# One head layout for the operands of the RWKV chunk products, halves exchanged by the stores, and a wider search for the issue order

## Chip, cores and metric

The kernel runs on one core of a Trainium2 chip. The time is the device time of one execution in microseconds. A core has five engines that run side by side, each through its own instructions in order: PE (TensorE, matmuls), DVE (VectorE), ACT (ScalarE), POOL (GpSimd) and SP (SyncE, which here only issues DMAs; ACT issues some too).

## The reference, cut to what matters

One decoder layer over T = 1024 tokens of width 1024, all in float32: a normalised input goes through one projection; its columns feed three head groups (8 RWKV-7 heads, 4 heads of sparse attention, 4 heads of attention over 256 memory tokens); their outputs go through one output projection.

```python
h = rms_norm(x, norm_in_g[l]); p = h @ w_in[l]
p_rwkv, p_nsa, p_mem = jnp.split(p, [...], axis=-1)
# RWKV-7, per head, token by token, S is a 64x64 state:
sa = jnp.einsum('bhvk,bhk->bhv', S, -kk_t)
S = (S * w_t[:, :, None, :] + sa[..., None] * (kk_t * a_t)[:, :, None, :]
     + v_t[..., None] * k_t[:, :, None, :])
y = jnp.einsum('bhvk,bhk->bhv', S, r_t)
# sparse attention and memory attention on their columns, then
x = x + jnp.concatenate([y_rwkv, y_nsa, y_mem], axis=-1) @ w_out[l]
return rms_norm(x, norm_final_g)
```

## The kernel before, in words

**Recording and ordering.** The program is written as generators. They don't issue instructions: `nc.vector`, `nc.tensor` and so on only record them. `ordered` then takes the whole list and chooses one order for all engines and queues, and issues it; every recorded instruction thus has the line of the call in `ordered` (L574). It goes through 30 turns. Each turn gives buffers to tiles in the order of the last turn (`_slots`), builds the dependences (`_edges`), ranks every instruction by the modelled time from it to the end (`_backward`), and lays the list out anew on modelled engines, highest rank first (`_forward`). The order whose modelled end is earliest is issued. At run time each engine follows its list strictly.

**Stages.** (1) x comes in as 8 tiles of 128 tokens (tiles `A_84` to `A_89`), is normalised and transposed into two halves `H`; a projection tile is `pa<-H,wh` and `pa<-H,wl`: 24 matmuls on a weight tile that was loaded raw (`wr`, one buffer), rounded by ACT (`wh`) and its rest taken by POOL or DVE (`wl`). (2) RWKV: `decay` and `elementwise` run for 8 units, head pair hp = 0 to 3 times half h of the tokens. Partitions 0 to 63 hold the even head of a pair, 64 to 127 the odd one. A unit makes xr (scaled kk and r, 128 columns for each of 8 chunks of 64 tokens) and bk (scaled b and k), multiplies them on PE head by head (64x128 tiles), masks the products into W and transposes bk into bt. All goes by DMA to `st_d` in DRAM, per chunk in four slots of 128 columns: 0 and 1 the operands for the state, 2 the chunk's own products, 3 bt. (3) `inverse(pr)` for head pairs 0, 1 (pr = 0, tile `A_336`) and 2, 3 (pr = 1, tile `A_480`): slot 2 is loaded as 128 small triangles, a substitution of 31 steps runs on DVE (a product `P4<-A` and a sum `A<-A,P4` each), ACT turns the result round, it goes through `md` and `nd` in DRAM, four passes of 32x32 matmuls join the triangles (pr = 1: `pa_539`, `pa_537`), and the result is stored to slot 2. (4) `chunks`: 16 chunks in sequence, each loading a 1 MB tile `C<-st_d`; per chunk PE makes px (`ch<-T,C`), ACT copies it (`xe`), PE makes pq (`ch<-xe,C`), DVE and ACT copy it, PE makes pn and DVE forms the next state. The first chunk is `ch_555<-T2_550,C_549`. Other work (memory attention, projections, sparse attention) is laid between these by the order. (5) The rest of the sparse attention and the output projection.

In the unit, the operands of the odd head have their two halves of 64 columns swapped (`halves`), so that each head's result lies on the partitions where the state needs it; all elementwise instructions there work on 64 partitions, and there are two masks, `MK[0]` and `MK[1]`.

Of the kernel before, what the change touches and what calls it, by code (L numbers as in the profile page):

```python
# [14 lines left out]
OP = mybir.AluOpType  # L15
# [382 lines left out]
def _backward(ops, preds, first):  # L398
# [15 lines left out]
    while done < n:  # L414
        best = None
        for e in engines:
            w, a = wait[e], able[e]
            while w and w[0][0] <= free[e]:
                k = heapq.heappop(w)[1]
                heapq.heappush(a, (-first[k], k))  # L420
            at = free[e] if a else w[0][0] if w else None
            if at is not None and (best is None or at < best[0]):
                best = at, e
        at, e = best
        if not able[e]:
            free[e] = at
            continue
        k = heapq.heappop(able[e])[1]
        o = ops[k]
        R[k] = max(floor[k], at + o.occ)  # L430
        free[e] = at + o.occ
        done += 1
        for p, same in preds[k].items():
            q = ops[p]
            d = 0.0 if same == 2 else q.occ if same else q.took + LAG[o.e] + MARGIN
# [8 lines left out]
def _forward(ops, preds, after, rank, phase):  # L444
# [20 lines left out]
    while done < n:  # L465
        if forced is not None:
            k, e, at = forced, "PE", free["PE"]
        else:
# [13 lines left out]
            if e == "PE" and prev is not None and len(able[e]) > 1:  # L482
                a = able[e]
                m = _mode(prev)
                k = min(a, key=lambda x: (x[0] + SWITCH * (_mode(ops[x[1]].shape) != m), x[1]))
# [55 lines left out]

MARGIN = 150.0
# [6 lines left out]
ROUNDS = 30  # L549


def ordered(tc, ops, log=None):
# [3 lines left out]
    seq = list(range(len(ops)))  # L556
    best, start = None, seq
    for n in range(ROUNDS):
        at = {k: n for n, k in enumerate(seq)}
# [3 lines left out]
        rank = _backward(ops, preds, start)  # L563
        rank = [r + max(0.0, FIRST - k) * 1e3 for k, r in enumerate(rank)]
        order, start, end = _forward(ops, preds, after, rank, 1100.0)
        if log is not None:
            log(n, late, end)
        seq = sorted(range(len(ops)), key=lambda k: (start[k], k))
        if best is None or end < best[0]:
            best = end, seq  # L570
# [9 lines left out]
def build(tc, x, mem, w_in, w_gl, w_kv, w_out, lora, pv_d, rows_d, cst_d, rope_d, w1_d, pos_d, w2_d, out):  # L580
# [3 lines left out]
    with ctx:  # L584
# [178 lines left out]
        MK = [maskb[:, K_MK + 128 * q:K_MK + 128 * q + 128] for q in range(2)]  # L763
# [180 lines left out]
        def elementwise(hp, h):  # L944
# [28 lines left out]
            halves = [(slice(64 * q, 64 * q + 64), 64 * q, 64 - 64 * q) for q in range(2)]  # L973
            for q, (r, ac, rc) in enumerate(halves):
                (V, G)[q].tensor_mul(xr[r, :, rc:rc + 64], r4[r], gg[r, :, 1:65])
                G.tensor_mul(bk[r, :, rc:rc + 64], p4_[r], gi4[r])
# [16 lines left out]
            for r, ac, rc in halves:  # L993
                V.scalar_tensor_tensor(xr[r, :, ac:ac + 64], k4[r], -1.0, gg[r, :, 0:64], op0=OP.mult, op1=OP.mult)
                V.scalar_tensor_tensor(bk[r, :, ac:ac + 64], b4[r], 0.5, gi4[r], op0=OP.mult, op1=OP.mult)
# [10 lines left out]
            for d in range(2):  # L1006
# [908 lines left out]
```

## Time and profile before

| | |
|---|---|
| time, median of 3 runs | 779.72 us (778.71 to 779.91) |
| profiled execution, its own time | 783.57 us |
| its span | 781.8 us |
| PE busy | 728.4 us, 93% |
| DVE, ACT, POOL busy | 540.4, 389.5, 342.6 us |
| DMA packets | 124744, of which 50816 under 512 B |

The profile is of one execution, 3.85 us longer than the median. An engine's busy share is over all stages; which wait counts in a stage is read from the idle time of PE there and what ended it. PEclk is the clock granted to PE, as a share of the full one.

### The profile page before, as it was taken

The numbers are of one execution on the slowest core, as the hardware profiler recorded it, in microseconds if no ns is written. First come the engines' busy times: TensorE is split into PE (matmuls) and PEld (weight loads), VectorE is DVE, ScalarE is ACT, GpSimd is POOL, SyncE is SP. The second block draws the span as 40 slices with busy tenths as digits, with TensorE's granted clock in tenths as the row PEclk, the third lists the DMA queues.
The fourth block names the chain that finished last, engine by engine and source line by source line (L and its number), as shares of the span: only waits on it lengthen the run. The fifth ranks groups of instructions, "written<-read, shape, count | busy, mean of one in ns | idle before, by whom it ended". The sixth has DMA issues, their size and how long they took to land.

```text
span 781.8 us, 15135 instructions
## 1 busy us (share of the span) xinstructions
PE 728.4 (93%) x5736; PEld 596.8 (76%) x5738; DVE 540.4 (69%) x1044; ACT 389.5 (50%) x854; POOL 342.6 (44%) x370
## 2 busy tenths in 40 slices
PE   2899999999999999779988999999998999999996
PEld 2888887888888878667766776777776888888885
DVE  4963658578888787744579868668898777666532
ACT  4653345263553222543567555453686675765541
POOL 3644416454273013120365656555243145255664
PEclk9999999999999998979999999999999999999998
DMA  8212574756757777598466675533251021121112
GB/s 338 77 32 62 124 191 105 179 133 176 190 128 192 207 160 123 164 163 281 150 203 203 195 243 178 176 109 106 91 162 61 8 75 36 54 81 62 55 55 80
DMA packets 124744, 105.67 MB, mean 135 GB/s; under 512 B 50816, under 2 KB 108544, under 8 KB 122496
## 3 DMA queue, kind: packets, MB, share of 16 engines
q1 hardware_dynamic: 108096, 95.57, 43.6%
q10 hardware_dynamic: 16576, 9.14, 4.3%
q8 instruction: 45, 0.74, 0.4%
q14 instruction: 27, 0.22, 0.1%
HBM read 68.52 MB, written 36.18 MB: 134 GB/s over the span
## 4 chain that ended last, share of the span: by engine, by line
PE 67%; DVE 12%; DMA 11%; ACT 3%; POOL 3%; issue 2%; SPq 0%; ACTq 0%; DVEq 0%; POOLq 0%
PE pa L574 47%; PE ch L574 20%; DVE A L574 4%; DVE T L574 2%; DMA A<-in_x_dram 2%; DMA yd<-S 2%; DVE S L574 1%; DVE P L574 1%; DVE wst L574 1%; DMA st_d<-A 1%; DMA S<-nd 1%; DMA C<-st_d 1%; DVE N L574 1%; DMA S<-g_d 1%; DMA wr<-in_w_out_dram 1%
## 5 line engine op out<-in xcount | busy, mean ns | idle before, releaser
L574 PE MATMUL pa<-H,wh 128*128 128x512 f32 (+1 forms) x928 | 292.5, 394 | 4.4 <-DVE H L574 1.7
L574 PEld LDWEIGHTS pa<-H,wh 128*128 128x128 f32 x928 | 170.7, 190 | 39.1 <-DVE H L574 2.1
L574 PE MATMUL pa<-H,wl 128*128 128x512 f32 (+1 forms) x464 | 180.6, 392 | 1.3 <-POOL wl L574 1.3
L574 POOL TENSOR_TENSOR wl<-wr,wh 128x1024 fp32r<-128x1024 f32 x27 | 66.1, 2447 | 104.6 <-ACT wh L574 96.2
L574 PE MATMUL ch<-H,C 128*128 128x512 f32 x360 | 104.4, 408 | 0.6 <-POOL H L574 0.4
L574 PEld LDWEIGHTS pa<-H,wl 128*128 128x128 f32 x464 | 88.1, 190 | 19.4 <-POOL wl L574 1.6
L574 ACT ACTIVATE S<-pa 128x512 fp32r<-128x512 f32 (+4 forms) x112 | 58.5, 544 | 44.6 <-PE pa L574 32.6
L574 PE MATMUL pa<-A 64*64 64x64 f32 (+4 forms) x416 | 74.6, 307 | 2.5 <-DVE A L574 1.7
L574 PEld LDWEIGHTS ch<-H,C 128*128 128x128 f32 x360 | 63.2, 189 | 9.7 <-POOL H L574 0.8
L574 ACT ACTIVATE wh<-wr 128x1024 fp32r<-128x1024 f32 x32 | 33.9, 1059 | 65.0 <-PE pa L574 43.1
L574 DVE TENSOR_REDUCE wst<-pa 128x1 f32<-128x384 f32 (+3 forms) x96 | 47.6, 516 | 16.4 <-PE pa L574 15.9
L574 PEld LDWEIGHTS pa<-A 128*128 128x128 f32 (+1 forms) x416 | 51.5, 175 | 9.2 <-issue 2.8
L574 DVE TENSOR_TENSOR N<-pa,S 128x512 fp32r<-128x512 f32 (+1 forms) x76 | 45.4, 615 | 13.0 <-ACT S L574 11.3
L574 PEld LDWEIGHTS ch<-T,C 128*64 128x64 f32 (+1 forms) x1008 | 33.6, 136 | 15.8 <-issue 6.2
L574 POOL TENSOR_TENSOR sgc<-T,gc 64x256 f32<-64x256 f32 x30 | 20.5, 683 | 56.3 <-DVE T L574 55.0
L574 PE MATMUL ch<-T,C 128*64 128x64 f32 (+1 forms) x1008 | 39.4, 226 | 5.0 <-ACT T L574 1.5
L574 DVE SCALAR_TENSOR_TENSOR T<-ch,gc,sgc 64x64 f32<-64x64 f32 x120 | 33.9, 283 | 13.1 <-PE ch L574 6.1
L574 ACT ACTIVATE T<-pa,pv 128x512 f32<-128x512 f32 x34 | 23.1, 681 | 34.3 <-PE pa L574 23.7
L574 ACT ACTIVATE NP<-pa,wst 128x384 f32<-128x384 f32 (+3 forms) x52 | 29.0, 564 | 19.2 <-DVE wst L574 10.9
L574 PE MATMUL pa<-cst,NP 128*128 128x128 f32 x212 | 33.6, 278 | 3.2 <-ACT NP L574 1.5
L574 POOL TENSOR_TENSOR S<-S,N 128x512 f32<-128x512 f32 x8 | 10.3, 1290 | 57.5 <-DVE N L574 39.1
L574 PEld LDWEIGHTS pa<-cst,NP 128*128 128x128 f32 x212 | 25.7, 142 | 9.6 <-ACT NP L574 2.8
(207 smaller groups left out, 1483.0 us busy)
## 6 DMA issues: line engine op xcount, KB each, us to landing
C<-st_d SPq DMA_DIRECT2D x16, 1024.0 KB, 5.6
wr<-in_w_in_dram SPq DMA_DIRECT2D x28, 512.0 KB, 3.9
st_d<-C SPq DMA_DIRECT2D x32, 256.0 KB, 4.7
st_d<-A SPq DMA_DIRECT2D x24, 256.0 KB, 3.6
A<-in_x_dram SPq DMA_DIRECT2D x8, 512.0 KB, 7.5
st_d<-NP SPq DMA_DIRECT2D x8, 512.0 KB, 5.5
P<-in_x_dram SPq DMA_DIRECT2D x8, 512.0 KB, 3.4
out_dram<-P SPq DMA_DIRECT2D x7, 512.0 KB, 2.6
```

The source lines that it names most:

```text
L574: i = o.call(*o.args, **o.kw).ins
```

## The change

In `elementwise`, xr and bk keep the same order of columns for both heads. Every 64-partition pair of instructions becomes one of 128 partitions: per unit, four multiplications (one on DVE, three on POOL) become two on POOL, and four scalar_tensor_tensor on DVE become two. One mask serves both heads. Since the products of the odd head then lie with halves swapped, the stores put them right: seven stores per unit become twelve, most of them of 64 columns (256 bytes in a row) where they were of 128 (512 bytes). The matmuls are the same in number and form.

In `ordered`, 150 turns replace 30. From turn 12 on, the ranks get random noise, the margin and the price of changing PE's tile size are drawn at random, and every second turn starts from the best order so far. What is best is judged no more by the modelled end of the layout but by `_replay`: the fixed order is played through the model three times with random slack on every duration, and the mean end counts.

```diff
@@ -546,28 +609,43 @@
-ROUNDS = 30
+ROUNDS = 150
+CHAIN = 12
+SEED = 0
+SPREAD = 0.06
+NOISE = 50.0
+AGAIN = 2
 
...
     users, tags = _tiles(ops)
-    seq = list(range(len(ops)))
-    best, start = None, seq
-    for n in range(ROUNDS):
-        at = {k: n for n, k in enumerate(seq)}
+    n, rng = len(ops), np.random.RandomState(SEED)
+    slacks = [(1 + SPREAD * np.abs(rng.randn(n)) * np.array([1 + 2 * (o.dma is not None) for o in ops])).tolist() for _ in range(3)]
+    seq = first = list(range(n))
+    best = None
+    for turn in range(ROUNDS):
+        if turn >= CHAIN and turn % AGAIN == 0:
+            seq, first = best[1], best[2]
+        at = [0] * n
+        for m, k in enumerate(seq):
+            at[k] = m
         taken = {t: sorted(names, key=lambda x: min(at[k] for k in users[x])) for t, names in tags.items()}
         took, late = _slots(users, taken, seq)
         preds, after = _edges(ops, users, took)
-        rank = _backward(ops, preds, start)
-        rank = [r + max(0.0, FIRST - k) * 1e3 for k, r in enumerate(rank)]
-        order, start, end = _forward(ops, preds, after, rank, 1100.0)
+        loose = turn >= CHAIN
+        add = NOISE * rng.randn(n) * loose
+        rank = _backward(ops, preds, first, MARGIN * (2 * rng.rand() if loose else 1.0))
+        rank = [r + max(0.0, FIRST - k) * 1e3 + a for (k, r), a in zip(enumerate(rank), add.tolist())]
+        order, start, end = _forward(ops, preds, after, rank, 1100.0, SWITCH * (2 * rng.rand() if loose else 1.0))
+        first, seq = start, sorted(range(n), key=lambda k: (start[k], k))
+        tries = [_replay(ops, preds, after, seq, 1100.0 * (m + 1), x) for m, x in enumerate(slacks)]
+        score = sum(x[0] for x in tries) / len(tries)
         if log is not None:
-            log(n, late, end)
-        seq = sorted(range(len(ops)), key=lambda k: (start[k], k))
-        if best is None or end < best[0]:
-            best = end, seq
+            log(turn, late, end, score)
+        if best is None or score < best[0]:
+            best = score, seq, first
     last = {}
     for k in best[1]:
         o = ops[k]
-        MK = [maskb[:, K_MK + 128 * q:K_MK + 128 * q + 128] for q in range(2)]
+        MK = maskb[:, K_MK:K_MK + 128]
         gc = const.tile([128, 4, 16], F32, name="gc")
...
             bk = NP((128, 8, 128))
-            halves = [(slice(64 * q, 64 * q + 64), 64 * q, 64 - 64 * q) for q in range(2)]
-            for q, (r, ac, rc) in enumerate(halves):
-                (V, G)[q].tensor_mul(xr[r, :, rc:rc + 64], r4[r], gg[r, :, 1:65])
-                G.tensor_mul(bk[r, :, rc:rc + 64], p4_[r], gi4[r])
+            G.tensor_mul(xr[:, :, 64:128], r4, gg[:, :, 1:65])
+            G.tensor_mul(bk[:, :, 64:128], p4_, gi4)
             yield 0.86, 0.0
 
             pvv = bank("ch")
...
             k4, b4 = ch(kn), ch(ba)
-            for r, ac, rc in halves:
-                V.scalar_tensor_tensor(xr[r, :, ac:ac + 64], k4[r], -1.0, gg[r, :, 0:64], op0=OP.mult, op1=OP.mult)
-                V.scalar_tensor_tensor(bk[r, :, ac:ac + 64], b4[r], 0.5, gi4[r], op0=OP.mult, op1=OP.mult)
+            V.scalar_tensor_tensor(xr[:, :, 0:64], k4, -1.0, gg[:, :, 0:64], op0=OP.mult, op1=OP.mult)
+            V.scalar_tensor_tensor(bk[:, :, 0:64], b4, 0.5, gi4, op0=OP.mult, op1=OP.mult)
             yield 0.43, L_BONUS
             pbn = bank("pa")
...
-                    V.tensor_mul(W[:, q, c4], pe[q], MK[q].unsqueeze(1).to_broadcast([128, 4, 128]))
+                    V.tensor_mul(W[:, q, c4], pe[q], MK.unsqueeze(1).to_broadcast([128, 4, 128]))
                 yield 1.1, L_MASK
-            for q in range(2):
-                r, o = slice(64 * q, 64 * q + 64), slice(64 - 64 * q, 128 - 64 * q)
-                nc.sync.dma_start(st_d[r, cl, 2, hp, :], W[r, q])
-                nc.sync.dma_start(st_d[o, cl, q, hp, :], W[o, q])
-                nc.sync.dma_start(st_d[r, cl, q, hp, :], xr[r])
-            nc.sync.dma_start(st_d[:, cl, 3, hp, :], bt)
+
+            u, d, both = slice(0, 64), slice(64, 128), (slice(0, 64), slice(64, 128))
+            nc.sync.dma_start(st_d[u, cl, 2, hp, :], W[u, 0])
+            nc.sync.dma_start(st_d[d, cl, 0, hp, :], W[d, 0])
+            nc.sync.dma_start(st_d[u, cl, 0, hp, :], xr[u])
+            for a, b in (both, both[::-1]):
+                nc.sync.dma_start(st_d[d, cl, 2, hp, b], W[u, 1, :, a])
+                nc.sync.dma_start(st_d[u, cl, 1, hp, b], W[d, 1, :, a])
+                nc.sync.dma_start(st_d[d, cl, 1, hp, b], xr[d, :, a])
+                nc.sync.dma_start(st_d[a, cl, 3, hp, d], bt[b, :, d])
+            nc.sync.dma_start(st_d[:, cl, 3, hp, u], bt[:, :, u])
 
         def rwkv():
             yield ("lora",)

```

The new `_replay` in its core:

```python
def _replay(ops, preds, after, seq, phase, slack):
    ...
    for k in seq:
        ...
        s = max(r, free[e])
        gap[k], why[k] = s - free[e], w if r >= free[e] else before[e]
        ...
        free[e], before[e] = c, k
        start[k], fin[k] = s, (s, f, c)
        if f > end:
            end, tail = f, k
    return end, gap, why
```

What the change does to the order is shown at three places. A name such as pa_562 is a PSUM tile; the number is the same in both kernels.

The first place is SP's queue at the start of the program, before:

```order
L574 DMA A_84<-in_x_dram 128x1024 x2
L574 DMA A_87<-in_x_dram 128x1024
L574 DMA wr_86<-in_w_in_dram 128x1024
L574 DMA A_87<-in_x_dram 128x1024
L574 DMA A_88<-in_x_dram 128x1024 x2
L574 DMA A_89<-in_x_dram 128x1024 x2
L574 DMA P4_152<-in_lora_dram 128x1024
L574 DMA wr_156<-in_w_in_dram 128x1024
```

and after:

```order
L652 DMA A_84<-in_x_dram 128x1024 x2
L652 DMA wr_86<-in_w_in_dram 128x1024
L652 DMA A_87<-in_x_dram 128x1024 x2
L652 DMA A_88<-in_x_dram 128x1024 x2
L652 DMA A_89<-in_x_dram 128x1024 x2
L652 DMA P4_152<-in_lora_dram 128x1024
L652 DMA wr_156<-in_w_in_dram 128x1024
```

The raw weight tile `wr_86` of the first projection now stands ahead of the third tile of x, not behind it. (A_87, A_88 and A_89 are the later pairs of tiles of x.)

The second place is PE at the four passes of 32x32 matmuls of the second inverse (`pa_539`, `pa_537`; `A_480` is its tile). Here is a piece of before, around the third and fourth pass (the first two stand further ahead in it, one in the midst of pa_562 and one in the midst of pa_548):

```order
L574 MATMUL pa_548<-H_104,wl_546 128x512
L574 MATMUL pa_548<-H_104,wh_547 128x512
L574 MATMUL pa_539<-A_480,S2_531 32x32 x32
L574 MATMUL pa_548<-H_105,wh_547 128x512
L574 MATMUL pa_548<-H_104,wl_546 128x512
L574 MATMUL pa_548<-H_104,wh_547 128x512
L574 MATMUL pa_537<-A_480,S2_530 32x32 x32
L574 MATMUL pa_548<-H_105,wh_547 128x512
L574 MATMUL pa_548<-H_104,wl_546 128x512
```

and of after:

```order
L652 MATMUL pa_603<-H_104,wh_588 128x512
L652 MATMUL pa_603<-H_105,wh_588 128x512
L652 MATMUL pa_603<-H_104,wl_587 128x512
L652 MATMUL pa_539<-S2_531,A_480 32x32 x32
L652 MATMUL pa_537<-S2_530,A_480 32x32 x32
L652 MATMUL pa_539<-A_480,S2_531 32x32 x32
L652 MATMUL pa_537<-A_480,S2_530 32x32 x32
L652 MATMUL pa_600<-A_524,A_532 128x256 x4
L652 MATMUL pa_608<-A_524,A_532 128x256 x4
L652 MATMUL pa_574<-cst_81,S2_569 128x128 x2
L652 MATMUL pa_610<-cst_81,NP_593 128x128
L652 MATMUL pa_591<-cst_81,S2_582 128x128 x2
```

The four passes now stand in one block, behind all 24 matmuls of the projection tile pa_603; in before the passes were spread between those of pa_562 and pa_548, and 22 of the 24 of pa_603 stood behind the first chunk. Between the last pass and the first chunk (`ch_555`) the new order has 21 matmuls of pa_589 and some small ones.

The third place is DVE near the end of the substitution of the second inverse. Before:

```order
L574 TENSOR_TENSOR P4_491<-A_480 128x87
L574 TENSOR_TENSOR A_524<-pa_529,A_524 64x256
L574 TENSOR_TENSOR A_480<-A_480,P4_491 128x29x3
L574 SCALAR_TENSOR_TENSOR A_532<-pa_538,A_532 64x512
L574 TENSOR_TENSOR P4_491<-A_480 128x60
L574 TENSOR_REDUCE mst_592<-pa_594 128x2
L574 TENSOR_TENSOR A_480<-A_480,P4_491 128x30x2
L574 SCALAR_TENSOR_TENSOR A_532<-pa_538,A_532 64x512
L574 TENSOR_TENSOR P4_491<-A_480 128x31
L574 SCALAR_TENSOR_TENSOR A_544<-pa_551,A_544 64x512
L574 TENSOR_TENSOR A_480<-A_480,P4_491 128x31
L574 RECIPROCAL mst_592<-mst_592 128x4
```

and after:

```order
L652 TENSOR_TENSOR A_480<-A_480,P4_491 128x26x6
L652 TENSOR_TENSOR P4_491<-A_480 128x135
L652 TENSOR_TENSOR wl_587<-wr_586,wh_588 128x1024
L652 TENSOR_TENSOR A_480<-A_480,P4_491 128x27x5
L652 TENSOR_TENSOR P4_491<-A_480 128x112
L652 TENSOR_TENSOR A_480<-A_480,P4_491 128x28x4
L652 TENSOR_TENSOR P4_491<-A_480 128x87
L652 TENSOR_TENSOR A_480<-A_480,P4_491 128x29x3
L652 TENSOR_TENSOR P4_491<-A_480 128x60
L652 TENSOR_TENSOR A_480<-A_480,P4_491 128x30x2
L652 TENSOR_TENSOR P4_491<-A_480 128x31
L652 TENSOR_TENSOR A_480<-A_480,P4_491 128x31
```

In before the steps of the loop alternate with memory attention's instructions up to the end. In after they run by themselves here, but the low part of a weight tile (`wl_587`, on DVE) stands inside the loop, so the nine instructions behind it can't start before `wh_588` is there.

## Rows read from the trace of the kernel before

**Rows 1.** The page, part 1: busy time, share of the span, instructions.

```profile
PE 728.4 (93%) x5736; PEld 596.8 (76%) x5738; DVE 540.4 (69%) x1044; ACT 389.5 (50%) x854; POOL 342.6 (44%) x370
```

**Rows 2.** Windows: from:to, length, busy time (count) by engine, PEclk, DMA share, GB/s.

```profile
40.00:280.00 240.00, 239.38 (x1328) 197.93 (x1327) 169.90 (x267) 98.22 (x151) 100.64 (x112) 1.00 0.57 143
280.00:368.00 88.00, 75.97 (x830) 62.85 (x828) 56.22 (x108) 32.30 (x66) 17.26 (x13) 0.90 0.80 174
368.00:518.00 150.00, 140.86 (x1822) 107.01 (x1822) 107.28 (x255) 83.72 (x195) 83.36 (x94) 1.00 0.60 190
...
337.00:347.50 10.50, 9.05 (x91) 8.04 (x91) 3.25 (x7) 3.20 (x9) 1.40 (x1) 0.51 1.33 199
```

**Rows 3.** PE's waits: waiting group, what ended the wait; total us, times, longest.

```profile
PE pa L574 <- ACT wh L574: 3.9, 3, 2.3
PE pa L574 <- POOL wl L574: 3.0, 2, 1.7
```

**Rows 4.** Timeline of PE at the start: start us, us, instructions [idle before <-releaser].

```profile
28.39 0.39 PE L574 MATMUL pa<-H,wh 128*128 128x256 f32 x1 [1.65 <-DVE H L574]
...
32.67 1.09 PE L574 MATMUL pa<-cst,A 128*128 128x128 f32 x8 [1.12 <-DVE A L574]
```

**Rows 5.** Groups by shape: busy us, mean ns of one | idle before. The edited instructions.

```profile
L574 POOL TENSOR_TENSOR NP<-A,N 64x512 f32<-64x512 f32 x16 | 24.1, 1503 | 6.2 <-PE ch L574 4.7 <-DVE A L574 0.6
...
L574 DVE SCALAR_TENSOR_TENSOR NP<-S,N 64x512 f32<-64x512 f32 x16 | 13.1, 818 | 0.1
...
L574 POOL TENSOR_TENSOR P<-P,S 128x512 f32<-128x512 f32 x8 | 10.7, 1333 | 10.2 <-ACT P L574 9.9 <-DMA S<-bv_d 0.2
```

**Rows 6.** Instructions that touch st_d: ns min/median/max, first and last start.

```profile
L574 SPq DMA_DIRECT2D st_d<-A x24: 551/586/1435, 83.6 to 355.4; - x24
```

**Rows 7.** Timeline of DVE, first and last step of the second inverse.

```profile
273.01 0.19 DVE L574 TENSOR_TENSOR P<-A 128x31 f32<-128x31 f32 x1 [3.14 <-DMA A<-st_d]
...
331.75 0.22 DVE L574 TENSOR_TENSOR A<-A,P 128x31 f32<-128x31 f32 x1
```

**Rows 8.** Timeline of PE: first passes of both inverses, last pass, first chunk.

```profile
290.40 0.22 PE L574 MATMUL pa<-S,A 32*32 32x32 f32 x2
...
342.59 1.92 PE L574 MATMUL pa<-S,A 32*32 32x32 f32 x64
...
352.64 1.20 PE L574 MATMUL pa<-A,S 32*32 32x32 f32 x64
...
368.36 1.15 PE L574 MATMUL ch<-T,C 128*64 128x64 f32 x32 [0.30 <-DMA C<-st_d]
```

**Rows 9.** Timeline of SP: raw weight loads of the single buffer.

```profile
298.07 0.35 SPq L574 DMA_DIRECT2D wr<-in_w_kv_dram  x1
...
310.78 0.54 SPq L574 DMA_DIRECT2D wr<-in_w_in_dram  x1
...
319.69 0.52 SPq L574 DMA_DIRECT2D wr<-in_w_kv_dram  x1
```

**Rows 10.** Timeline of PE: first products that use a new low part.

```profile
318.82 0.50 PE L574 MATMUL pa<-H,wl 128*128 128x512 f32 x1 [1.27 <-POOL wl L574]
319.15 0.62 PE L574 MATMUL pa<-H,wh 128*128 128x512 f32 x2
319.62 0.40 PE L574 MATMUL pa<-H,wl 128*128 128x512 f32 x1
319.85 0.62 PE L574 MATMUL pa<-H,wh 128*128 128x512 f32 x2
```

**Rows 11.** Groups by shape: low parts on POOL and on DVE.

```profile
L574 POOL TENSOR_TENSOR wl<-wr,wh 128x1024 fp32r<-128x1024 f32 x27 | 66.1, 2447 | 104.6 <-ACT wh L574 96.2 <-PE pa L574 8.2
...
L574 DVE TENSOR_TENSOR wl<-wr,wh 128x1024 fp32r<-128x1024 f32 x5 | 6.1, 1225 | 3.5 <-ACT wh L574 3.5
```

**Rows 12.** Timeline of PE: px and pq of the eleventh chunk.

```profile
455.47 1.15 PE L574 MATMUL ch<-T,C 128*64 128x64 f32 x32 [0.49 <-ACT P L574]
...
457.80 0.68 PE L574 MATMUL ch<-xe,C 64*64 64x64 f32 x16
```

More of the change, by code (lines that the diff above doesn't have):

```diff
@@ L395, in block, with _backward @@
     return n
-def _backward(ops, preds, first):
+def _backward(ops, preds, first, margin):
     n = len(ops)
@@ L434, in _backward @@
             q = ops[p]
-            d = 0.0 if same == 2 else q.occ if same else q.took + LAG[o.e] + MARGIN
+            d = 0.0 if same == 2 else q.occ if same else q.took + LAG[o.e] + margin
             floor[p] = max(floor[p], R[k] + d)
@@ L441, in _backward, with _forward @@
     return R
-def _forward(ops, preds, after, rank, phase):
+def _forward(ops, preds, after, rank, phase, switch):
     n = len(ops)
@@ L484, in _forward @@
                 m = _mode(prev)
-                k = min(a, key=lambda x: (x[0] + SWITCH * (_mode(ops[x[1]].shape) != m), x[1]))
+                k = min(a, key=lambda x: (x[0] + switch * (_mode(ops[x[1]].shape) != m), x[1]))
                 a.remove(k)
@@ L539, in _forward @@
     return order, start, end
+def _replay(ops, preds, after, seq, phase, slack):
+    n = len(ops)
+    ready, why, start, gap = [700.0] * n, [-1] * n, [0.0] * n, [0.0] * n
+    free, before = dict.fromkeys(LAG, 700.0), dict.fromkeys(LAG, -1)
+    member = set(after.values())
+    lanes, port, holder, server = [0.0] * LANES, 0.0, "", 0.0
+    slow, busy, prev, pe_at, pe_occ, end = True, 0.0, None, 0.0, 0.0, 0.0
+    fin = [None] * n
+    for k in seq:
+        o = ops[k]
+        e = o.e
+        x = slack[k]
+        r, w = 700.0, -1
+        for p, same in preds[k].items():
+            a, f, c = fin[p]
+            t = a if same == 2 else c if same else f + LAG[e]
+            if t > r:
+                r, w = t, p
+        if e == "PE" and k in member:
+            r = 0.0
+        s = max(r, free[e])
+        gap[k], why[k] = s - free[e], w if r >= free[e] else before[e]
+        if e == "PE":
+            if prev is not None:
+                if _mode(o.shape) != _mode(prev) and s < pe_at + pe_occ + 100:
+                    s = max(s, pe_at + pe_occ + 100 * (1 + slow))
+                a1 = min(s, pe_at + pe_occ)
+                w0 = int((pe_at + phase) // WINDOW)
+                e1 = (w0 + 1) * WINDOW - phase
+                share = 0.5 if prev[1] == 32 else 0.85 if prev[1] == 64 else 1.0
+                busy += (min(a1, e1) - pe_at) * share
+                w1 = int((s + phase) // WINDOW)
+                if w1 > w0:
+                    slow = busy < 0.5 * WINDOW or slow and busy < 0.8 * WINDOW
+                    busy = max(0.0, a1 - e1) * share
+                    if w1 > w0 + 1:
+                        slow, busy = slow or busy < 0.5 * WINDOW or w1 > w0 + 2, 0.0
+            pe_at, prev = s, o.shape
+            pe_occ = o.occ * (1 + slow)
+            c = s + pe_occ
+            f = s + o.took * (1.5 if slow else 1.0)
+        elif o.dma:
+            issue, l0, serve, l1 = o.dma
+            lane = min(range(LANES), key=lambda y: lanes[y])
+            s = max(s, lanes[lane])
+            server = max(server, s + issue + l0) + serve * x
+            f = server + l1 * x
+            lanes[lane] = f
+            c = s + o.occ
+        else:
+            t, c = o.took * x, o.occ * x
+            if o.lock:
+                y = max(0.0, port - s) if holder != e else 0.0
+                t, c, port, holder = t + y, c + y, s + t + y - 30, e
+            f, c = s + t, s + c
+        free[e], before[e] = c, k
[3 more added lines that the diff above has]
+    return end, gap, why
```

## The prediction, made before the changed kernel was run

> **What bounds the kernel now.** I read the page's first part, then the windows by stage, then PE's waits and its timeline where it idles, and last the queues that end these waits. The reader should see first that PE is busy for 93% of the span [rows 1], and then that this share is an average over stages of three kinds. From 40 to 280 us, where all eight units of `elementwise` run, PE is busy 239.38 of 240 us: nothing that DVE, POOL or a queue does there can give time back, except by what it hands to the next stage. From 280 to 368 us, the stage of the two inverses, PE idles 12 of 88 us and its mean clock is 0.90; in the stretch 337 to 347.5 us, just after waits, it is 0.51, that is the lower of its two levels (1.2 against 2.4 GHz) nearly throughout [rows 2]. From 368 to 518 us, the 16 chunks, PE is busy 140.86 of 150 us [rows 2]. The waits of the inverse stage are for weight tiles, `wh` 3.9 us and `wl` 3.0 us in all [rows 3], and behind them stands the one raw buffer `wr`. The stage ends when `C<-st_d` lands and the first chunk starts, at 368.36 [rows 8].
>
> **The sum's base.** The durations come from the profiled execution, 783.57 us with a span of 781.8; the median is 3.85 us below it. I sum differences against the span and apply them to the median, 779.72. A measurement of this kernel can tell about 0.2%, 1.6 us, from no change.
>
> **The layout edit, directly: 0.** A half-width instruction took 1503 ns on POOL and 818 ns on DVE; the nearest full-width row on POOL takes 1333 ns [rows 5], so the 24 halves of xr and bk on POOL and the 8 on DVE become 16 on POOL, and 32 scalar_tensor_tensor on DVE become 16. POOL saves some 10 us in all and DVE some 20, but all of it between 85 and 260 us, where PE has no hole [rows 2]. I take 0. If PE were waiting there for the units, up to 2 us a unit would come back, 16 us in all; the full PE excludes that.
>
> **The stores: 0, at most 4 us.** SP issues 40 stores more, five per unit, and one takes about 0.6 us [rows 6]: 3 us of queue per unit. For seven units the full PE covers it. For the last one, what is queued behind its twelve stores is the loading of the second inverse's triangles (`A_480<-st_d`), whose lateness DVE already waited for, 3.14 us [rows 7]. There it would cost 3 to 4 us if the inverse started from this load; below I find that another chain is longer, so I take 0. The page "DMA: Bandwidth & Descriptors" of the Trainium skill, section "Specifications", says that transfers under 512 bytes don't reach line rate because they are done by read-modify-write, and it speaks against the 256-byte halves. The trace of before has no store of that width to show it; by that rule the stores would also land later, and the last rival below would cost more.
>
> **The start: -1.2 us.** Before, PE waits 1.65 us at 28.39 and 1.12 us at 32.67, the second for the transposes of a later x tile [rows 4]. In the new order the first weight tile is loaded one place earlier, and products of the next projection stand ahead of those transposes. I take the second wait as covered, 1.1 us, and 0.1 of the first. Bounds: both vanish, -2.8; the x tile that is now loaded after the weight is waited for, +1.5.
>
> **The inverse stage: -3.5 us.** Followed from the order, with before's durations:
> - The first pass of 32x32 products of the first inverse stood at 290.40 [rows 8]. It keeps its place in PE's work to within 0.5 us; with the start's gain it comes at 288.7. Its inverse is ready much earlier now, since its loop ends on DVE before the second one's starts, so PE needn't wait there. The second passes follow after some 3.5 us, DVE's copies end at 293.5, and two stores of 0.6 to 1 us each lead the next raw weight tile (`wr_540`) to 295.3, against 298.07 before [rows 9].
> - From then on four raw tiles follow through one buffer. Before, a tile took 318.82 - 310.78 = 8.0 us from its issue to the first product with its low part, and the next was issued 8.9 us after it [rows 9, 10]. With 8.0 each, `wr_586` is issued at 295.3 + 4 x 8.0 = 327.3. Its low part is now made by DVE, 1.2 us instead of 2.4 [rows 11]: ready at 334.1.
> - That instruction stands inside the second inverse's loop. Nine instructions are left behind it, some 0.25 us each: the loop ends at 336.6, against 331.97 before [rows 7]. The queue behind it on DVE is only the loop; PE waits for both.
> - Before, 10.6 us went from the loop's end to the first pass (331.97 to 342.59), and 14.5 us from the last pass's end to the first chunk (353.84 to 368.36) [rows 7, 8]. With the same spans the first pass comes at 347.2, and the four passes of 1.2 us, now in one block, with two copies of 0.7 end at 352.7 or so; the first chunk starts at 367.2, 1.2 us earlier than before.
> - PE has done more by then: 22 of the matmuls of pa_603 and 10 of pa_589 more, less 4 wide ones, 8 of 256 columns and 14 of 128 that now come later. A wide one takes 0.23 us (three from 319.15 to 319.85 in [rows 10]), one of 256 columns 0.12, one of 128 some 0.1: 28 x 0.23 - 8 x 0.12 - 14 x 0.1 = 4.0 us of work that the chunks' stage is rid of.
> - Against that: between the last pass and the first chunk only 6.4 us of work stand, so PE idles some 8 us, and at least 4 ahead of the first pass. After idle time the clock was low for 10 us before [rows 2]. If the first 7 us of the chunks run at the lower level, that is 3.5 us lost; if the clock is back by then, as before at 368, none. I take half, 1.7.
>
> The page "TensorE: Matmul & The Clock Gate" of the Trainium skill says in Part 1 that an idle PE falls to 1.2 GHz; the 0.51 of rows 2 agrees. -1.2 - 4.0 + 1.7 = -3.5 us. Bounds: with DVE alone as the limit -9 (below), with the slower buffer +5.5 (below).
>
> **The chunks: +1.5 us.** Between px and pq PE needs cover while ACT copies: at the eleventh chunk pq came 1.18 us after px's end, which work filled (455.47 + 1.15 to 457.80) [rows 12], and I take that as the least. In the new order the cover there is 0.44, 0.79, 0.87 and 0.81 us in the third and the fifth to seventh chunk, by counting the matmuls between; with two thin places before the next px, 3.8 us are missing, against 0.8 before. So +3.0 directly; but PE idles 9.1 us in this stage now [rows 2], and the work that left these places covers others. I take half; bounds -5 and +5. What follows the chunks keeps its order nearly: 0, within 3.
>
> **Sum.** -1.2 + 0 + 0 - 3.5 + 1.5 = -3.2 us, 776.5.
>
> **Rivals.**
> - **Faster, 768.5.** The raw tiles come quicker than 8.0 us each, and DVE alone limits the loop. Before, the loop took 59 us [rows 7]; I count 11 us of waits in DVE's timeline there, which leaves 0.45 us for each of its 106 instructions; now 93 stand from about 290 on, which makes 332. The first chunk then starts at 362.6: -5.8 - 4.0, with half of the clock's price, 0.8, is -9.0; the chunks gain 1 instead of losing, the start keeps 1.2: -11.2. For it: 1.2 us tiles on DVE and no other load between them on SP. Against: the buffer's 8.0 to 8.9 us in the trace.
> - **Slower, 785.5.** One mechanism, the low part inside the loop. If each tile takes 8.9 us and the chain starts at 298.07, as before, `wr_586` is issued at 333.7, the loop ends at 343.9 and the first chunk starts at 374.5: +6.1 - 4.0, and the low clock in full, 3.4, is +5.5; with start and chunks +5.8. It decides from a first chunk at 370.4, a loop that ends at 339.8.
> - **No change, 780.5.** The 4.0 us of work done earlier give nothing, because the chunks are set by their own chain of px, xe, pq, pn and not by PE's work: -1.2 - 1.2 + 1.7 + 1.5 = +0.8. For it: the thin covers. Against: PE is busy 94% there.
> - **The stores count after all, 780.** The last unit's twelve stores delay the triangles by 3.5 us and the loop starts late: -3.2 + 3.5 = +0.3.
>
> **Chances.** Forecast 0.34 (its own range 773 to 779.5), faster rival 0.24, slower 0.22, no change 0.14, stores 0.06. Faster by over 0.2%: 0.34 x 0.85 + 0.24 + 0.02 = 0.55; within: 0.34 x 0.12 + 0.12 + 0.04 = 0.20; slower 0.25. The range goes from 766, a little under the faster rival, to 787, a little over the slower one.
>
> **What would show it.** Right: no wait of PE at the first inverse's passes; raw tiles 8 us apart from 295 on; `wl_587` near 334 with the loop's last nine instructions right behind it; the first chunk near 367 with about 4 us more work done; PE busy under 138 us in the chunks' stage, and that stage shorter than 149. DVE some 20 us and POOL some 10 us less busy, PE's 40 to 280 still full. Wrong: a first chunk after 370, a chunks' stage as long as before, or a hole in PE between 85 and 260 us. What could upset all of it is that the first 250 us no longer keep PE full, which would show as waits for `C` or `A` of the units.

## The result and the profile after

790.18 us (median of four runs, 789.49 to 793.46) against 779.82 for the kernel before on the same chip (four runs, 778.71 to 784.12): a ratio of 1.013, 95% interval 1.008 to 1.018. The change makes the kernel 10.4 us slower; 776.5 was predicted, in a range of 766 to 787. In the profiled execution (789.74 us, span 788.0) the first part of the page reads, against [rows 1]:

```profile
PE 729.0 (93%) x5736; PEld 600.1 (76%) x5738; DVE 513.2 (65%) x1020; ACT 389.3 (49%) x854; POOL 332.9 (42%) x362
```

PE's busy time is the same; DVE is busy 27 us less (some 20 were priced) and POOL 10 us less, and it buys nothing. The windows, against [rows 2]:

```profile
40.00:280.00 240.00, 240.00 (x1329) 197.90 (x1328) 141.85 (x233) 101.49 (x153) 89.30 (x106) 1.00 0.64 146
280.00:368.00 88.00, 67.41 (x710) 57.71 (x710) 52.11 (x101) 23.43 (x42) 16.65 (x11) 0.85 0.67 150
```

Up to 280 us nothing is lost. In the inverse stage PE idles 20.6 us (before 12.0) and its mean clock is 0.85 (before 0.90). What it waits for there, from its waits between 280 and 385 us (total us, times, longest):

```profile
PE pa L652 <- DMA S<-nd: 8.1, 2, 6.8
PE pa L652 <- DVE S L652: 7.3, 1, 7.3
PE pa L652 <- ACT wh L652: 1.7, 1, 1.7
```

Two waits that before does not have are most of it: one for DVE's copies of the first inverse, one for the second inverse's matrix coming back from `nd` (before waits once for `nd`, 1.9 us, and that is for the first inverse). PE's timeline has them, and the first chunk, against [rows 8]:

```profile
288.39 2.28 PE L652 MATMUL pa<-S,A 32*32 32x32 f32 x128
...
299.44 3.87 PE L652 MATMUL pa<-A,S 32*32 32x32 f32 x128 [7.28 <-DVE S L652]
...
361.85 0.28 PE L652 MATMUL pa<-S,A 32*32 32x32 f32 x2 [6.76 <-DMA S<-nd]
363.50 3.62 PE L652 MATMUL pa<-S,A 32*32 32x32 f32 x126 [1.37 <-DMA S<-nd]
...
382.84 1.15 PE L652 MATMUL ch<-T,C 128*64 128x64 f32 x32 [1.14 <-DMA C<-st_d]
```

The first passes come at 288.39 as predicted (288.7), without a wait. The second ones wait 7.28 us, and after each long wait a pair of passes takes 3.6 to 3.9 us where a pair took 2.28 at 288.39: the clock has fallen. The granted clock is 1.00 from 288.39 to 290.67, and 0.50, the lower level of 1.2 GHz, from 299.44 to 303.31 and from 361.85 to 370.50. The first chunk starts at 382.84, 14.5 us later than before. From there to the end 405.2 us go by (to 788.0), against 413.4 before (368.36 to 781.8). 14.5 - 8.3 = 6.2 us is the difference of the two spans. It is less than 10.4 because the profiled execution of before was itself 3.75 us over its median (783.57 for 779.82) and that of the change 0.44 under; the two traces account for the 6.2.

Why the copies were late stands in DVE's timeline, against [rows 7]:

```profile
253.37 1.29 DVE L652 TENSOR_TENSOR C<-pa,maskb 128x512 f32<-128x512 f32 x2 [1.06 <-PE pa L652]
...
274.44 1.28 DVE L652 TENSOR_TENSOR C<-pa,maskb 128x512 f32<-128x512 f32 x2
...
297.52 0.19 DVE L652 TENSOR_TENSOR P<-A 128x31 f32<-128x31 f32 x1 [13.09 <-DMA A<-st_d]
297.75 0.68 DVE L652 COPY S<-pa 32x512 f32<-32x512 f32 x1
...
350.37 0.21 DVE L652 TENSOR_TENSOR A<-A,P 128x31 f32<-128x31 f32 x1
```

The four mask products of the last unit fall apart: two at 253.4, two at 274.4. Before, the last of the eight that start between 225 and 290 us starts at 259.7 (ns min/median/max, first and last start):

```profile
L574 DVE TENSOR_TENSOR C<-pa,maskb x8: 675/680/690, 233.1 to 259.7; 128x512 f32<-128x512 f32 x8
```

The second inverse's first step stands ahead of the copies on DVE, and it sits there for 13.09 us because a load of its triangles hasn't landed; the copies, and PE behind them, wait too. SP's timeline shows why the load is so late:

```profile
276.99 2.41 SPq L652 DMA_DIRECT2D st_d<-C  x2
...
282.88 1.68 SPq L652 DMA_DIRECT2D A<-st_d  x2
284.61 1.95 SPq L652 DMA_DIRECT2D st_d<-C  x3
286.66 0.58 SPq L652 DMA_DIRECT2D g_d<-T  x1
287.28 1.27 SPq L652 DMA_DIRECT2D T<-sv_d  x2
288.65 0.55 SPq L652 DMA_DIRECT2D P<-in_rope_dram  x1
289.24 0.97 SPq L652 DMA_DIRECT2D A<-st_d  x2
...
306.98 0.60 SPq L652 DMA_DIRECT2D wr<-in_w_kv_dram  x1
318.01 0.34 SPq L652 DMA_DIRECT2D wr<-in_w_in_dram  x1
```

The same queue before:

```profile
259.45 3.80 SPq L574 DMA_DIRECT2D st_d<-C  x4
263.35 2.28 SPq L574 DMA_DIRECT2D A<-st_d  x2
...
267.65 1.05 SPq L574 DMA_DIRECT2D A<-st_d  x2
```

The stores wait for the masks, the loads for the stores, and the last pair of loads stands at 289.24 behind four other transfers (`g_d`, two of `sv_d`, the rope table), 21.6 us later than before. The raw weight tile that was predicted at 295.3 is issued at 306.98.

### The profile page after: what moved, and what is told of

It reads as the page before. It is cut to its first block, busy times and chain, and to the rows that moved or that the text cites. A ratio compares the mean times of both kernels' runs of the same rounds, so it can differ in the third digit from the quotient of the medians.

```text
span 788.0 us, 15132 instructions
## 1 busy us (share of the span) xinstructions
PE 729.0 (93%) x5736; PEld 600.1 (76%) x5738; DVE 513.2 (65%) x1020; ACT 389.3 (49%) x854; POOL 332.9 (42%) x362
## 4 chain that ended last, share of the span: by engine, by line
PE 73%; DVE 10%; DMA 6%; ACT 4%; issue 3%; SPq 2%; POOL 1%; ACTq 0%; DVEq 0%; POOLq 0%
PE pa L652 53%; PE ch L652 20%; DVE A L652 2%; DMA S<-nd 2%; DVE T L652 2%; SPq L652 2%; DVE wst L652 2%; DVE S L652 1%; DMA S<-in_cst_dram 1%; ACT A L652 1%; DMA A<-st_d 1%; DVE N L652 1%; DVE st L652 1%; DVE P L652 1%; ACT S L652 1%
## 5 line engine op out<-in xcount | busy, mean ns | idle before, releaser
L652 PE MATMUL pa<-H,wh 128*128 128x512 f32 (+1 forms) x928 | 297.7, 400 | 3.2 <-ACT wh L652 1.9
L652 PEld LDWEIGHTS pa<-H,wh 128*128 128x128 f32 x928 | 173.2, 193 | 38.6 <-ACT wh L652 2.3
L652 PE MATMUL ch<-H,C 128*128 128x512 f32 x360 | 107.6, 412 | 0.1
L652 PEld LDWEIGHTS pa<-H,wl 128*128 128x128 f32 x464 | 89.0, 192 | 19.5 <-DVE wl L652 2.1
L652 PE MATMUL pa<-A 128*128 128x256 f32 (+4 forms) x416 | 76.9, 307 | 1.2 <-DVE N L652 1.1
L652 ACT ACTIVATE NP<-pa,wst 128x384 f32<-128x384 f32 (+3 forms) x52 | 29.1, 563 | 20.6 <-DVE wst L652 16.4
L652 PE MATMUL pa<-cst,NP 128*128 128x128 f32 x212 | 36.6, 276 | 1.1 <-ACT NP L652 0.8
L652 DVE TENSOR_TENSOR P<-A 128x31 f32<-128x31 f32 (+15 forms) x62 | 24.9, 402 | 18.7 <-DMA A<-st_d 17.3
L652 DVE TENSOR_TENSOR C<-pa,maskb 128x512 f32<-128x512 f32 x32 | 21.0, 685 | 24.2 <-PE pa L652 24.2
L652 PE MATMUL ch<-N,A 128*128 128x256 f32 x132 | 32.4, 305 | 0.9 <-DVE N L652 0.9
```

The source lines that it names most:

```text
L652: i = o.call(*o.args, **o.kw).ins
```

## The experiments

Thirteen kernels were run, first against three theories: A, the place of the second inverse makes the loss, by the late masks and by its first step ahead of the copies on DVE; B, the stores do by themselves; C, the wider search finds a worse order. Later ones are D, the layout makes the planner place the last unit late in every order; F, the late unit is a matter of the draw of the search's random numbers; G, that unit's place is what costs the time, and H, it only goes with a bad order; W and X, which part of the layout turns it. Times are medians; ratios are against the kernel before on the same chip (780.97 to 782.13 us there). "Last masks" is the start of the last mask product of the eight units, "first chunk" that of the first chunk, both in the profiled execution.

| kernel | us | ratio, 95% | last masks | first chunk |
|---|---|---|---|---|
| before | 779.82 | | 259.7 | 368.4 |
| the change (seed 0) | 790.18 | 1.008 to 1.018 | 275.0 | 382.8 |
| layout_only | 799.40 | 1.017 to 1.024 | 277.5 | 385.9 |
| search_only | 762.59 | 0.971 to 0.978 | 246.7 | 353.7 |
| pin_dve | 790.13 | 1.006 to 1.013 | 274.5 | 378.8 |
| pin_dve_sp | 786.50 | 1.004 to 1.008 | 274.5 | 377.7 |
| before_split | 784.04 | 1.001 to 1.005 | 261.0 | 369.6 |
| split_stores | 780.72 | 0.996 to 1.000 | 255.4 | 361.1 |
| after_seed1 | 768.41 | 0.977 to 0.986 | 250.9 | 352.0 |
| after_seed2 | 793.52 | 1.012 to 1.018 | 271.0 | 383.3 |
| after_seed9 | 771.63 | 0.984 to 0.990 | 256.6 | 353.6 |
| search_only_seed1 | 772.30 | 0.986 to 0.990 | 248.0 | 359.4 |
| early_unit | 768.39 | 0.980 to 0.984 | 244.7 | 351.3 |
| late_unit | 784.22 | 1.002 to 1.007 | 276.7 | 365.4 |
| narrow_ops | 780.50 | 0.995 to 1.000 | 255.8 | 363.3 |

### The two halves of the change

layout_only is the change with the functions `_backward`, `_forward` and `ordered` of before; search_only is the kernel before with those of the change.

> The layout edit and its stores, ordered by the search of before (30 turns, judged by the modelled end). Three theories. A, the place of the second inverse: it is slow because the last unit's masks stand 15 us later in PE's work and the first step of the second inverse's loop stands ahead of the first inverse's copies on DVE; this order has both as well, so 784 to 792 us. B, the stores: forty stores more, of 256-byte rows, make the triangles late; 784 to 792 too. C, the wider search picks an order that is only good in the model: with the old search 776 to 782.

> The layout and stores of before, ordered by the new search. In this order the last unit's masks stand at 210 us of PE's work (218.6 before, 233.4 in the changed kernel). A: 770 to 782 us, since the second inverse's triangles come early. B: the same, as there are no more stores. C: 786 to 794.

The wider search alone makes the kernel 19.5 us faster; the layout alone makes it 17.3 us slower. The search is not to blame, and the layout, with the order that it gets, costs far more than the 0 of the prediction. Both kernels with the changed layout have the last masks late; layout_only has them late with before's search, which draws no random numbers. Both times lie 7 us outside theory A's ranges, layout_only over and search_only under.

### The two places on DVE and SP

pin_dve takes the change's order and moves, on DVE, the second inverse's steps behind the first one's copies; pin_dve_sp also moves, on SP, the other transfers behind the last pair of triangle loads:

```diff
+    moved = [k for k in seq[:end] if ops[k].e == "DVE" and out(k)[0] in ("P4_491", "A_480")]
...
+    seq = keep[:end] + moved + keep[end:]
+    loads = [k for k in seq if ops[k].e == "SP" and out(k) == ["A_480"]][4:8]
...
+    moved = [k for k in seq[a:b] if ops[k].e == "SP" and out(k) != ["A_480"] and src(k)[:1] != ["C_452"]]
```

> The changed kernel's order with one thing moved: the steps of the second inverse's loop that stood among the first inverse's copies on DVE come behind them. A: PE's wait of 7.3 us for these copies goes, the copies (5.5 us) fill DVE's wait for the triangles, the loop ends some 5 us earlier, first chunk near 377: 784 to 787 us. B: the loop still starts near 297.5 and the chain behind it is as long; at most 2 us of gain, 788 to 791.

> As pin_dve, and on SP the second pair of the triangles' loads stands ahead of a 512 KB load and of small loads that nobody waits for yet. A: the loads are issued at 287 instead of 289.2 and land 3 to 5 us earlier, the loop starts near 293; 780 to 784 us. B: as pin_dve, 787 to 791, because the stores ahead of them set their landing.

In pin_dve the wait is gone, PE's timeline against that of the change:

```profile
287.82 2.28 PE L666 MATMUL pa<-S,A 32*32 32x32 f32 x128
291.51 1.57 PE L666 MATMUL pa<-A,S 32*32 32x32 f32 x87
...
358.10 3.72 PE L666 MATMUL pa<-S,A 32*32 32x32 f32 x128 [5.81 <-DMA S<-nd]
```

The second passes come 7.9 us earlier, the second inverse only 3.8. The time is that of the change to 0.1 us; set against before on its own chip, pin_dve is 8.0 us over it and the change 10.4, and the two intervals overlap, so a gain isn't shown. That fits B's range and not A's. With SP mended as well the kernel takes 786.50 us, 3.7 less than the change, or 6.0 less when each is set against before on its own chip (4.4 over it), between the ranges of A and B. The two places are real and not the whole: the last masks stay late (274.5), and the rest of the loss with them. That the waits are links of a chain which starts at the masks is argued here, not shown.

### The stores

before_split is the kernel before in its own order to the instruction, with four of each unit's seven stores cut where they are issued: by its edit three are cut in two and one, that of bt, in three, not five in two as its expectation says. It makes the same twelve, nine of them with 256-byte rows. split_stores is search_only with twelve stores that the planner knows of:

```diff
-                nc.sync.dma_start(st_d[r, cl, 2, hp, :], W[r, q])
...
+                for c in ((slice(0, 128),), (slice(0, 64), slice(64, 128)))[q]:
+                    nc.sync.dma_start(st_d[r, cl, 2, hp, c], W[r, q, :, c])
```

> The kernel before in its own order to the instruction, except that five of each unit's seven stores are cut in two where they are issued: twelve stores with 256-byte rows in the place of seven with 512-byte rows. This is the direct price of the stores, with no planner in between. B: 785 to 790 us (5 to 10 us over before). F and D: 778 to 782 us (at most 2 us over before).

> The elementwise operations and the layout of before, with the wider search (seed 0), and each unit's seven stores cut into twelve, as many as in the change and with the same 256-byte rows, but without an exchange of halves. B (stores cost by themselves) and D (they make the planner place the unit late): 782 to 792 us, against 762.6 us for the wider search with seven stores. F (the draw): the search's own estimate is 757.7 us here (743.5 us with seven stores), so 776 to 781 us; the difference to 762.6 us is then one of order, and seed 1 of the changed kernel, with the same twelve stores, shows that they can be had for nothing.

The stores cost 2.6 us (0.07 to 0.49%, that is 0.5 to 3.8 us) when nothing else changes: the second inverse's first step moves from 273.01 to 275.08 and the first chunk from 368.36 to 369.63. That is less than theory B wanted and 2 us over the range of F and D, and within the bound of the prediction, "at most 4". before_split has both kinds of the same tile's store; the page's list of issues (times, size of one, median us to landing):

```profile
st_d<-C SPq DMA_DIRECT2D x16, 256.0 KB, 4.0
st_d<-C SPq DMA_DIRECT2D x32, 128.0 KB, 3.1
```

The first have 512-byte rows, the second 256-byte rows: half the bytes take three quarters of the time (in before, where all 32 stores of this tile are of the first kind, they take 4.7). The page "DMA: Bandwidth & Descriptors" of the Trainium skill, section "Specifications", gives 512 bytes as the least for full rate. The rows would fit that, and a fixed part in each transfer as well; either way it is a matter of 2.6 us here. split_stores is 18.1 us slower than search_only, though, and not by the stores' price: its order is another, with the last masks 8.7 us later.

### The draw

The mean end that `_replay` gives for the order that is issued is called the estimate here. Three kernels change the seed alone, `SEED = 1`, `2` or `9` for 0; search_only_seed1 is search_only with seed 1.

> The changed kernel with one number changed: the seed of the random numbers that the wider search draws is 1 in place of 0. Every instruction, every store and every tile is that of the changed kernel; the order alone is another. Theory F (the draw): the layout costs next to nothing, and the 790 us of seed 0 is an unlucky order, in which the last triangle unit lies late. The search's own estimate of the order that it picks is 739.1 us for this seed, 767.1 us for seed 0, and 743.5 us for the wider search on the old layout, which ran in 762.6 us; the two that ran took 19 to 23 us more than their estimates, so F expects 758 to 762 us here, with the last unit's masks done on DVE before 265 us (275.7 with seed 0) and the first chunk at 352 to 362 us (382.8 with seed 0). Theory B (the twelve stores with 256-byte rows cost by themselves, in SP's queue and on the DMA engines): 780 us or more with any seed. Theory D (the dearer stores make the planner place the last unit late): 780 to 795 us with any seed, masks after 272 us.

> The changed kernel with seed 2. The search's own estimate of its order is 766.2 us, against 767.1 us with seed 0. Theory F (the draw) expects it as slow as seed 0: 785 to 793 us. Theories B and D expect 780 to 795 us as well, so this run tells by itself only whether the estimate orders the kernels: with F alone the two seeds with an estimate of 766 to 767 us lie within 5 us of each other, and seed 1 lies 25 us under both.

> The changed kernel with seed 9, a further draw whose estimate is low (740.3 us). F and G: last masks before 260 us and 762 to 770 us in all. With seed 1 (768.4 us) it also says whether the changed layout is as fast as the old one when both have an early last unit (762.6 us): if the layout itself costs 4 to 6 us, as the gap of seed 1 suggests, this run lies at 766 us or more; if it costs nothing, at 760 to 765 us.

> The wider search on the old layout with seed 1 (estimate 751.1 us, against 743.5 us with seed 0, which ran in 762.6 us). It gives the spread of the draw on the old layout: F and G expect an early last unit again (last masks before 256 us) and 768 to 774 us. Under 764 us, the estimate does not order two kernels that both have the unit early; over 780 us, the old layout can be unlucky as well.

The same instructions, with the same stores, take 768.4, 771.6, 790.2 or 793.5 us. In after_seed1 the four masks stand together, and the second inverse's first step waits 1.36 us where it waited 13.09; DVE's timeline:

```profile
249.08 2.47 DVE L652 TENSOR_TENSOR C<-pa,maskb 128x512 f32<-128x512 f32 x4
...
262.37 0.19 DVE L652 TENSOR_TENSOR P<-A 128x31 f32<-128x31 f32 x1 [1.36 <-DMA A<-st_d]
```

Theories B and D fall in the form that they were given, 780 us or more with any seed: with seeds 1 and 9 the layout is 13.0 and 9.5 us faster than before, and its masks are early. A price of a few us of the layout itself is not excluded by that, as the wider search gains 9 to 20 us with the old layout too. Seed 9, at 771.6, spoke by its expectation for a price of 4 to 6 us; search_only_seed1, at 772.3, takes that back, since the old layout spreads as far (762.6 and 772.3) with early masks. Four draws of one layout and two of the other can't settle it. after_seed1 and after_seed9 came 6 and 2 us over their ranges and after_seed2 0.5 over its: the estimate tells the late orders of these seeds from the early ones, and places a kernel to some 10 us.

### The place of the last unit

```diff
+        rank = [r + UNIT * (k in unit) for k, r in enumerate(rank)]
         order, start, end = _forward(ops, preds, after, rank, 1100.0, SWITCH * (2 * rng.rand() if loose else 1.0))
```

`unit` holds the steps that the last unit's stores need and no earlier unit's do. early_unit has `UNIT` = 24000 (ns) and seed 0, late_unit -32000 and seed 1.

> The changed kernel, seed 0, with one rule added to the search: in every pass the steps of the last triangle unit (its elementwise work, its products and masks, its twelve stores) rank 24 us earlier than the planner's backward pass gives. Instructions and stores are those of the changed kernel. Theory G (the place of the last unit in the order decides; seed 0 is slow because its second pair of masks lies at 275 us): the last masks start before 256 us, the first chunk at 350 to 358 us, 763 to 774 us in all (the search's own estimate is 744.8 us, and the runs so far took 19 to 29 us more than theirs). Theory H (the late unit only goes with a bad order, and does not make it): 780 to 793 us although the masks are early.

> The counterpart: the changed kernel with seed 1, which ran in 768.4 us, and the last unit's steps ranked 32 us later in every pass. G: the last masks start after 268 us, the first chunk after 374 us, 784 to 793 us in all (estimate 762.6 us). H: 764 to 776 us, as with seed 1.

early_unit takes 768.4 us, 21.8 less than the change with the same seed; its masks, the group of them between 225 and 290 us (ns min/median/max, first and last start):

```profile
L673 DVE TENSOR_TENSOR C<-pa,maskb x8: 676/679/690, 236.2 to 244.7; 128x512 f32<-128x512 f32 x8
```

late_unit is 15.8 us slower than seed 1, just inside G's range, but not by G's path alone. Its first chunk starts at 365.4, not after 374, and PE has a hole ahead of the inverses that the change does not have; its windows:

```profile
220.00:240.00 20.00, 16.30 (x86) 13.56 (x86) 14.27 (x28) 7.10 (x12) 8.44 (x9) 0.83 0.75 187
240.00:260.00 20.00, 12.61 (x62) 10.21 (x60) 4.72 (x11) 5.49 (x6) 4.40 (x4) 0.82 1.13 211
```

So early_unit and the seeds carry the conclusion, and late_unit only half supports it. In early_unit too the search runs on from the changed ranks, so more than the one place differs: that the order makes the loss is shown, that the last unit's place is what matters in it is shown in part.

### What in the layout turns the order

narrow_ops is the change with one layout, twelve stores and the exchange, but with eight elementwise operations of 64 partitions in a unit in place of four of 128:

```diff
-            G.tensor_mul(xr[:, :, 64:128], r4, gg[:, :, 1:65])
...
+            for q, r in enumerate((slice(0, 64), slice(64, 128))):
+                (V, G)[q].tensor_mul(xr[r, :, 64:128], r4[r], gg[r, :, 1:65])
```

> The changed kernel, seed 0, with its one layout, its twelve stores and its exchange of halves; only the four elementwise operations of a unit that the change made 128 partitions wide are again eight of 64 partitions each, on the engines that they had before. Theory W (the wide operations turn the search to a late last unit; stores and layout don't): the last masks start before 262 us, the first chunk before 366 us, 776 to 784 us in all, near the 780.7 us of the old layout with twelve stores (the estimates of the two orders are 757.5 and 757.7 us). Theory X (the exchange of the halves, or the layout itself, turns it): last masks after 270 us and 786 to 794 us, as with the change.

```profile
L652 DVE TENSOR_TENSOR C<-pa,maskb x8: 676/682/692, 231.9 to 255.8; 128x512 f32<-128x512 f32 x8
```

The last masks are back at 255.8 and 9.7 us of the 10.4 are gone, as theory W expected. The stores and the exchange alone thus needn't lead to a late unit. That the wide operations, the part that saves DVE and POOL their 37 us of work, tip the search is not shown: it draws one number for each instruction (`rng.randn(n)`), narrow_ops has 32 instructions more, and so seed 0 is another draw for it. Two of the four seeds of the change have early masks with the operations wide. The same holds for search_only and split_stores beside the change.

## Why the prediction was wrong, by its steps

- **"The layout edit, directly: 0."** Right as far as it goes: 40 to 280 us stayed full, DVE and POOL lost the work that was priced. What failed is the word directly: the edit changes what the planner is given, and layout_only shows that even before's search answers with another order (last masks at 277.5 for 259.7).
- **"The stores: 0, at most 4 us."** The direct price is 2.6 us (before_split). The last rival, "the stores count after all", had the right place, the triangles' load ahead of the second inverse, and the wrong size: it put the delay at 3.5 us. The load was waited for 13.09 us, because the masks ahead of the stores were 15 us late and four other transfers stood between; the second inverse's first step came 24.5 us later than before (297.52 for 273.01). Their order could be read before the run, and the prediction took their time from before. It also says that before has no store with 256-byte rows. It has eight, the `st_d<-A` that store the inverses' results between 303 and 355 us: the first four landed in 4.6 us and the last four in 6.4 (medians), against 3.6 for the sixteen of the same size with 512-byte rows earlier on. They ran beside other transfers, so this doesn't price the rows either.
- **"PE needn't wait there", "DVE's copies end at 293.5".** This is the step that failed: the second inverse's start, taken as early. The second inverse's first steps had moved ahead of the copies on DVE; their own start was taken as early since the loop before them ends early, and the load that they need was not followed. The raw tile came at 306.98 for 295.3, the loop ended at 350.58 for 336.6, 14.0 us late.
- **What follows the loop** held: 11.3 us to the first pass (10.6 taken), 21.0 from there to the first chunk (20.0 taken). With the 14.0 these make the 15.6 us by which the first chunk missed 367.2. The clock was 0.50 up to 370.5 and 0.66 on the mean from there to the first chunk; in the first 10 us of the chunks it was 1.00, so the 1.7 that was taken for it there was 0.
- **"Tiles 8.0 us apart", `wl_587` as the loop's last wait.** 11.0 us from the first to the second (306.98 to 318.01), then 8.3. `wl_587` was not waited for: DVE came to it at 346.97 after 0.16 us of idle time. The loop was set by DVE itself from 297.52 on, as the faster rival had it, but from a start 7.5 us later, and it took 53.1 us where the rival's 93 instructions of 0.45 us make 42. Of the 53.1, DVE was idle for 2.7, and 7.5 went into five steps that were held up by POOL (last section). By time the slower rival, 785.5, is the nearest; its mechanism, the low part inside the loop, is not what happened.
- **The start and the work done earlier.** -1.2 and -4.0 were predicted. PE was busy 1.7 us more in the first 40 us (24.43 for 22.71, from the windows), and 3.2 us less in the chunks' stage (137.26 for 140.47). Both were right in sign. The sum, though, counts the start twice: the first chunk at 367.2 was reached from 288.7, which has the 1.2 us in it, and then -1.2 was added again. Without that the prediction is -2.0 us, 777.7; the miss stays.
- **The chunks, +1.5:** the stage, from the first chunk to the end of the last chunk's last `ch<-T,C`, took 147.7 us (382.84 to 530.50) for 149.3 before (368.36 to 517.67). The thin covers cost nothing that shows: the stage is 1.6 us shorter, where -4.0, +1.7 and +1.5 together had it 0.8 shorter.
- **What follows the chunks, "0, within 3":** 257.5 us (530.50 to 788.0) for 264.1 (517.67 to 781.8), 6.6 us less, outside the bound. PE was busy 2.9 us less there and idle 3.7 us less. Why isn't known, and some of it may belong to the slower execution of before that was profiled. With the 1.6 it hid 8.3 of the 14.5 us; nothing in the prediction called for it.

What stays open: what in the layout, if anything, leads seed 0 and before's search to the late masks. That the search starts again from its best order in every second of its later rounds may hold it there; no run tried that. The place of the last unit isn't all either: split_stores and narrow_ops take 9 us more than after_seed9, whose last masks are no earlier (256.6) but whose first chunk is 7.5 and 9.7 us earlier, and late_unit lost its time in another place.

## What to carry to other kernels

Where a search sets the order, an edit is first a new draw: compare several seeds of both kernels before a difference of 3% is put down to the edit. When the order of a changed kernel can be read, follow each first step of a stage back to its load, and the load to the work that writes it, with the new order's times and not with those of the trace before. A saved 37 us on engines that aren't waited for can be worth nothing, or worse than nothing, if the edit that saves it moves what is.

## What the runs showed of the hardware

A loop step on DVE that takes 0.4 us elsewhere took over 2 us twice in the second inverse. DVE's timeline of the change:

```profile
331.79 2.04 DVE L652 TENSOR_TENSOR A<-A,P 128x252 f32<-128x252 f32 x1
...
338.96 2.30 DVE L652 TENSOR_TENSOR A<-A,P 128x220 f32<-128x220 f32 x1
```

POOL's timeline of the same stretch:

```profile
331.14 2.41 POOL L652 TENSOR_TENSOR wl<-wr,wh 128x1024 fp32r<-128x1024 f32 x1 [4.85 <-ACT wh L652]
338.62 2.39 POOL L652 TENSOR_TENSOR wl<-wr,wh 128x1024 fp32r<-128x1024 f32 x1 [5.07 <-ACT wh L652]
```

Each long step ends 0.3 us after a low part on POOL (333.55 and 341.01) ends. The Trainium skill's page "Trainium Architecture — The Big Picture", section "What this means for kernel authors", says that DVE and GpSimd share one port pair to SBUF under an exclusive lock; the two rows agree, with some 1.6 and 1.9 us for one collision. It is in DVE's time and not in the low part's. All five low parts that POOL made during the loop held up one step each (the others took 1.82, 1.70 and 1.54 us), 7.5 us in all over what steps of these widths take elsewhere. An instruction of DVE that reads PSUM was not held: a copy `A<-pa` at 303.19 took 0.67 us, as usual, beside the low part of 303.02 to 305.48. The prediction has no term for it; the 0.45 us of the faster rival is a mean in which before's own collisions are contained (a step at 296.10 took 2.23 us).
